# Moving the attention of the first query block into the gate stage of the second token group

## The chip, the cores and the metric

The kernel runs on one core of a Trainium2 chip. A core has five engines with an instruction queue each: TensorE (PE, matrix products), VectorE (DVE), ScalarE (ACT), GpSimd (POOL) and SyncE (SP, which issues nearly all DMAs here). Each engine takes its instructions in the order in which the program lists them, and waits on semaphores of the others. The metric is the device time of one execution in microseconds (us), and less is better.

## The reference

The reference is one step of a decoder of two layers on 2048 prompt tokens and a small sample group of 64 tokens. Each layer reads one modulated input `h`, makes four branches from it, multiplies each by its own gate, and sends all through one output product:

```python
z = h @ w_in[l]
aq, ak, av, ag, bu, bv, bg, cin, cg, dq, df, di, dg = jnp.split(z, SPLITS, axis=-1)
...
p = probs(q1, k1) - lam * probs(q2, k2)           # A: differential attention, causal, 4 heads
o_a = rms_norm(p @ v) * silu(ag)
o_c = silu(layer_norm(conv31(glu(cin)))) @ w_pw * silu(cg)   # C: depthwise convolution, 31 taps
...
mixed = jnp.concatenate([o_a, o_b, o_c, o_d], -1) @ w_out[l]
y = layer_norm(ALPHA * x + gate * mixed)
```

Branch A is the attention that the change moves. Branch C matters because its taps and its norm share the stage to which the attention is moved. Branches B (a spatial gate) and D (a linear recurrence) are untouched.

## The kernel before

A layer runs in two parts. The first part goes over the tokens in two groups of 1024, `g` = 0 and 1. For a group it makes all products with `w_in` (TensorE, three products per piece since each operand is split into a high and a low half; lines L516 to L518 and L525 to L527, accumulators `z`), keys, queries and values among them, which go to memory. The last stretch of a group is called the gate stage here: products for the gates (`gate_b`, `gate_slab`, `gate_pair`; 24 products and one `gate2` on VectorE, L195, per tile), while VectorE does the 31 taps of the convolution (`c_taps`, L1026), and then the two norms of branch C, one per 512 tokens (`c_norm`: transposes L1040, statistics L1042 to L1047, scaling L1050, transposes back L1055, tanh L1058, VectorE L1059, product L1065). In layer 0 the gate stage of `g` = 1 also makes the modulation vectors of layer 1 (`mod`, L291 to L311), whose accumulator is the single bank `X`.

The second part is the attention stage. It goes over blocks of query tiles: tiles 0 to 3, 4 to 7, 8 to 11, then 12 and 13, then 14 and 15. They are called blocks 0 to 4. `attention` loads V, and for each of four heads K and Q; for each query tile it makes two score tiles (`S`, L678), their maxima on VectorE (L682), exponentials on ScalarE (L686), the difference of the two on VectorE (L712), transposes (`T`, L725), copies (`ph`, L727) and the product with V (`X`, L730). At the end of a head ScalarE copies the sum out (`asb`), PE turns it (L741), VectorE norms it, POOL multiplies it (`ms`, L756), and it is stored in `cat`. Block 0 has 1 to 4 key tiles for its query tiles, so it is the cheapest.

The output product needs `w_out` split into two halves: `out_weights` loads sixteen pieces (`raw`, 128 x 512), ScalarE casts each (`woh`, L1306), POOL subtracts (`wol`, L172). It writes where `h` was, so it can't begin before the last product that reads that part of `h`. `out_tile` makes one tile of 128 tokens (L1354 transposes, L1373 to L1375 products, `z`); the tile of the 64 sample tokens is made first.

The order on each engine is set when the program is built: a list scheduler with its own clock takes instructions by priority, and memory that a pool gives back can be taken by the next pool as soon as its last reader is done. Nothing is reordered on the chip. The two norms have a high priority, and the order of calls in the gate stage is the string `ORD1 = 'g8 n2'`: eight gate tiles, then both norms, then the rest. `attention` draws on pools with five buffers of K, two of Q, and five and three of the exponentials.

Of the kernel before, what the change touches and what calls it, by code (L numbers as in the profile page):

```python
# [9 lines left out]
F32 = mybir.dt.float32  # L10
F32R = mybir.dt.float32r
# [13 lines left out]
P = 128  # L25
# [43 lines left out]
def hymba_step_kernel(  # L69
# [16 lines left out]
    NG = T // TG  # L86
# [8 lines left out]
              POUT=-500, PATT=0, PMOD=0, PW=0, PAV=0, PDZ=3000, PQK=500, PSL=0, PSLD=0, PPR=0, PPB=0, OT=1, GO=0, DO=0,  # L95
# [3 lines left out]
    def prio(o, f, *a):  # L99
        if not o:  # L100
            return f(*a)
        with tc.high_priority(o):
            return f(*a)
# [8 lines left out]
    NK, NMW, NPH, NP1, NP2, LEAD = (KN[k] for k in ('NK', 'NMW', 'NPH', 'NP1', 'NP2', 'LEAD'))  # L112
# [17 lines left out]
    pool = L()  # L130
# [3 lines left out]
    def nm(s):  # L134
        uid[0] += 1
        return f"{s}_{uid[0]}"
# [28 lines left out]
    def load(out, in_):  # L165
        return nc.sync.dma_start(plain(out), in_)  # L166
# [70 lines left out]
    for l in range(DEPTH):  # L237
        t = cp.tile([P, npg], I32, name=f"pidx{l}")
# [391 lines left out]
    def attention(l, t0, nt, Lx, ap, act=None):  # L630

        S = scr[l]
        prev = None
        gq, oq = divmod(t0 * P, TG)
        nkc = -(-(t0 + nt) // 4)
        while len(pool.vst) < nkc:
            vt = (ap.v if pool.vst else ap.v0).tile([P, 4, 256], F32, name=nm("V"))
            load(vt, S.vs[len(pool.vst)].rearrange("(k p) c -> p k c", p=P))
            pool.vst.append(vt)
        vst = pool.vst  # L640
        for hd in range(4):
            rows = slice(hd * 64, (hd + 1) * 64)
            kst = []
            for c in range(0, nkc * 512, 512):
                gg, o = divmod(c, TG)
                kt = ap.k.tile([P, 2, 512], F32R, tag="K", name=nm("K"), bufs=NK)
                for q, part in enumerate((0, 0, 1, 1)):
                    load(kt[q * 32:(q + 1) * 32], S.ks[gg][part][rows, o:o + 512].rearrange("(m d) t -> d m t", m=2))
                kst.append(kt)
            qt = ap.q.tile([P, 2, 512], F32R, tag="Q", name=nm("Q"), bufs=2)  # L650
            for q, part in enumerate((0, 1, 0, 1)):
                load(qt[q * 32:(q + 1) * 32, :, 0:nt * P], S.qs[gq][part][rows, oq:oq + nt * P].rearrange("(m d) t -> d m t", m=2))
            ls = smp.tile([P, 4], F32, tag="ls", name=nm("ls"), bufs=3)
            acc = None
            for j in range(nt):
                pm = prio(KN['PPB'] if t0 else KN['PPB'], attn_probs, t0 + j, qt[:, :, j * P:(j + 1) * P], kst, ls[:, j:j + 1], Lx, ap)
                if prev is not None:
                    prio(KN['PAV'], prev)
                acc = Xt() if j == 0 else acc
                prev = (lambda *a: lambda: attn_value(*a, Lx, l, ap))(t0 + j, pm, vst, acc, ls, j, nt, hd, act)  # L660
        prev()

    def attn_probs(qi, qt, kst, l1, Lx, ap):

        nk = qi + 1
        npc = -(-nk // 8)
        stt = smp.tile([P, 16], F32, tag="stt", name=nm("stt"), bufs=3)
        Pm = []
        sizes = [min(8, nk - k0) * P for k0 in range(0, nk, 8)]
        col = lambda m, j: stt[:, m * 8 + j:m * 8 + j + 1]  # L670
        for m in range(2):
            pms = []
            for pc, n in enumerate(sizes):
                s = St()
                for o in range(0, n, 512):
                    w = min(512, n - o)
                    diag = pc == npc - 1 and o + 512 >= n
                    nc.tensor.matmul(s[:, o:o + w], qt[:, m, :], kst[pc * 2 + o // 512][:, m, 0:w], start=True, stop=not diag)  # L678
                    if diag:
                        nc.tensor.matmul(s[:, o + w - P:o + w], identb, cmaskb, start=False, stop=True)  # L680

                nc.vector.tensor_reduce(col(m, pc), s[:, :n], AX.X, ALU.max, negate=True)  # L682
                if pc:
                    nc.vector.tensor_tensor(col(m, pc), col(m, pc), col(m, 0), ALU.min)  # L684
                p = (ap.p1, ap.p2)[m].tile([P, 1024], F32, tag=("P1", "P2")[m], name=nm("P"), bufs=(NP1, NP2)[m])
                nc.scalar.activation(p[:, :n], s[:, :n], AF.Exp, bias=col(m, pc), scale=1.0, accum_out=l1 if m == 0 and npc == 1 else col(m, 2 + pc))  # L686
                pms.append(p)
            lt = l1 if m == 0 and npc == 1 else col(m, 2)
            if npc > 1:

                nc.scalar.activation(col(m, 5), col(m, 0), AF.Exp, bias=col(m, 1), scale=-1.0)
                lt = col(m, 6) if m else l1
                nc.vector.scalar_tensor_tensor(lt, col(m, 2), col(m, 5), col(m, 3), op0=ALU.mult, op1=ALU.add)
            Pm.append((pms, lt))
        (p1s, lt1), (p2s, lt2) = Pm
        r = col(0, 7)
        nc.vector.reciprocal(r, lt2)
        nc.vector.scalar_tensor_tensor(r, lt1, Lx.nlam, r, op0=ALU.mult, op1=ALU.mult)
        for pc, n in enumerate(sizes):
            p1, p2 = p1s[pc], p2s[pc]  # L700
            if pc == 0 and npc > 1:
                nc.vector.tensor_tensor(col(1, 7), col(1, 5), r, ALU.mult)
                if KN['EP2']:
                    nc.gpsimd.tensor_scalar(p2[:, :n], p2[:, :n], col(1, 7), None, op0=ALU.mult)
                else:
                    nc.scalar.activation(p2[:, :n], p2[:, :n], AF.Copy, scale=col(1, 7))
                nc.vector.scalar_tensor_tensor(p1[:, :n], p1[:, :n], col(0, 5), p2[:, :n], op0=ALU.mult, op1=ALU.add)  # L707
            elif n <= KN['ECB'] * P:
                nc.scalar.activation(p2[:, :n], p2[:, :n], AF.Copy, scale=r)
                nc.gpsimd.tensor_tensor(p1[:, :n], p1[:, :n], p2[:, :n], ALU.add)  # L710
            else:
                nc.vector.scalar_tensor_tensor(p1[:, :n], p2[:, :n], r, p1[:, :n], op0=ALU.mult, op1=ALU.add)  # L712
        return p1s
# [582 lines left out]
    def out_weights(l, op):  # L1296

        O = L()
        O.op = op
# [101 lines left out]
    Lx = mod_begin(0)  # L1401
# [7 lines left out]
    for l in range(DEPTH):  # L1409
        with ExitStack() as ctx2:  # L1410
# [3 lines left out]
            for g in range(NG):  # L1414
# [38 lines left out]
                with tc.tile_pool(name=nm("cn"), reuse_waits="tile", bufs=1) as C.pool:  # L1453
# [30 lines left out]
                    for what in ORD1 if g == NG - 1 else ORD0:  # L1484
                        if what[0] == "g":
                            step(gp, int(what[1:]))
                        elif what[0] == "n":
                            norms(int(what[1:]))
                        else:
                            step(bh, int(what[1:]))  # L1490
# [11 lines left out]
        with ExitStack() as ctx2, \  # L1502
                tc.tile_pool(name=nm("pz"), reuse_waits="tile", bufs=1, space=PSUM) as pool.z, tc.tile_pool(name=nm("pT"), reuse_waits="tile", bufs=1, space=PSUM) as pool.T2:
            ap = L()
            for n in APO:
                setattr(ap, n, ctx2.enter_context(tc.tile_pool(name=nm("ap" + n), reuse_waits="tile", bufs=1)))
            op = ap.op
            if KN['WF']:
                O = prio(KN['PW'], out_weights, l, op)

            qbs = [(t, 4) for t in range(0, NT - 4, 4)] + ([(NT - 4, 2), (NT - 2, 2)], [(NT - 4, 3), (NT - 1, 1)], [(NT - 4, 2), (NT - 2, 1), (NT - 1, 1)])[KN['QB']]
            pool.vst = []
            for i, qb in enumerate(qbs):
                act = op.tile([P, qb[1], 256], F32, name=nm("act")) if i == len(qbs) - 1 else None
                if i and KN['OT'] == 0:
                    for t in range(qbs[i - 1][1]):
                        prio(KN['POUT'], out_tile, l, qbs[i - 1][0] + t, O)
                prio(KN['PATT'], attention, l, *qb, Lx, ap, act)
                if i == 0:
                    if not KN['WF']:  # L1520
                        O = prio(KN['PW'], out_weights, l, op)
                    out_gate(l, O, True)
                    out_tile(l, None, O)
                    out_gate(l, O, False)
                elif KN['OT']:
                    for t in range(qbs[i - 1][1]):
                        prio(KN['POUT'], out_tile, l, qbs[i - 1][0] + t, O)
            for t in range(qbs[-1][1]):
                out_tile(l, qbs[-1][0] + t, O, True, act[:, t])
        pool.T2 = None  # L1530
# [4 lines left out]
        Lx = NX[0]  # L1535
# [39 lines left out]
```

## Time and profile before

| | |
|---|---|
| timed, median of 3 runs | 3167.21 us (3165.14 to 3172.83) |
| the profiled execution | 3160.83 us, span 3159.1 us |
| PE busy | 2828.0 us, 90% of the span |
| VectorE busy | 2235.2 us, 71% |
| ScalarE busy | 1162.9 us, 37% |
| POOL busy | 960.8 us, 30% |

The timed runs and the profiled execution are different runs; the profiled one is 6.4 us under the median. Shares are means over the whole span. The change touches two short stretches, around 1020 us (layer 0) and around 2550 us (layer 1), so the views are read there. In a row of a timeline the first number is the start in us and the second the duration; `x4` means four instructions shown together; the square brackets give how long the engine sat idle before it, and what it waited for.

### The profile page before, as it was taken

The numbers are of one execution on the slowest core, as the hardware profiler recorded it, in microseconds if no ns is written. First come the engines' busy times: TensorE is split into PE (matmuls) and PEld (weight loads), VectorE is DVE, ScalarE is ACT, GpSimd is POOL, SyncE is SP. The second block draws the span as 40 slices with busy tenths as digits, with TensorE's granted clock in tenths as the row PEclk, the third lists the DMA queues.
The fourth block names the chain that finished last, engine by engine and source line by source line (L and its number), as shares of the span: only waits on it lengthen the run. The fifth ranks groups of instructions, "written<-read, shape, count | busy, mean of one in ns | idle before, by whom it ended". The sixth has DMA issues, their size and how long they took to land. (4 is left out here: it accounts for less than half of the span.)

```text
span 3159.1 us, 55749 instructions
## 1 busy us (share of the span) xinstructions
PE 2828.0 (90%) x20888; PEld 2254.7 (71%) x20888; DVE 2235.2 (71%) x5280; ACT 1162.9 (37%) x2452; POOL 960.8 (30%) x1061
## 2 busy tenths in 40 slices
PE   5999989898999798888979999999999988997986
PEld 3888876788876566656668888767888856665665
DVE  2567883367583788879956678833676749898897
ACT  3212223211112666666641112232110146567663
POOL 3344364312011233404253344552120031332232
PEclk8999999899999899989989999999999988998998
DMA  6433544323555754446453335444334355444652
GB/s 237 147 128 108 173 146 154 108 92 128 174 180 203 184 133 112 118 112 166 122 197 111 122 119 192 140 139 124 117 120 140 117 166 123 129 118 108 158 155 67
DMA packets 323263, 441.31 MB, mean 140 GB/s; under 512 B 58704, under 2 KB 207734, under 8 KB 315811
## 3 DMA queue, kind: packets, MB, share of 16 engines
q1 hardware_dynamic: 316850, 420.97, 44.0%
q0 software_dynamic: 6144, 16.79, 1.8%
q8 instruction: 165, 2.70, 0.4%
q14 instruction: 104, 0.84, 0.1%
HBM read 295.80 MB, written 142.05 MB: 139 GB/s over the span
## 5 line engine op out<-in xcount | busy, mean ns | idle before, releaser
L525 PE MATMUL z<-hh,wh 128*128 128x512 f32 (+1 forms) x1440 | 528.4, 367 | 17.1 <-DVE zs L195 9.1
L527 PE MATMUL z<-hh,wl 128*128 128x512 f32 (+1 forms) x1440 | 522.1, 363 | 0.0
L526 PE MATMUL z<-hl,wh 128*128 128x512 f32 (+1 forms) x1440 | 518.6, 360 | 0.0
L516 PE MATMUL z<-wh,hh 128*128 128x256 f32 (+1 forms) x1360 | 399.9, 294 | 16.0 <-ACT wh L110 4.3
L686 ACT ACTIVATE P<-S,stt 128x1024 f32<-128x1024 f32 (+7 forms) x384 | 332.7, 868 | 182.1 <-DVE stt L682 120.0
L518 PE MATMUL z<-wh,hl 128*128 128x256 f32 (+1 forms) x1360 | 394.7, 290 | 0.0
L517 PE MATMUL z<-wl,hh 128*128 128x256 f32 (+1 forms) x1360 | 393.9, 290 | 0.6 <-POOL wl L172 0.6
L682 DVE TENSOR_REDUCE stt<-S 128x1 f32<-128x1024 f32 (+7 forms) x384 | 344.0, 904 | 64.2 <-PE S L680 48.7
L1026 DVE SCALAR_TENSOR_TENSOR acc<-glu,cw,acc 128x512 f32<-128x512 f32 x480 | 378.0, 834 | 3.3
L525 PEld LDWEIGHTS z<-hh,wh 128*128 128x128 f32 x1440 | 275.7, 191 | 80.1 <-issue 14.4
L527 PEld LDWEIGHTS z<-hh,wl 128*128 128x128 f32 x1440 | 275.5, 191 | 44.7 <-issue 7.0
L526 PEld LDWEIGHTS z<-hl,wh 128*128 128x128 f32 x1440 | 275.7, 191 | 42.7 <-issue 6.3
L678 PE MATMUL S<-K,Q 128*128 128x512 f32 (+3 forms) x640 | 229.2, 430 | 77.1 <-ACT P L686 61.6
L516 PEld LDWEIGHTS z<-wh,hh 128*128 128x128 f32 (+1 forms) x1360 | 262.3, 193 | 25.9 <-issue 5.7
L517 PEld LDWEIGHTS z<-wl,hh 128*128 128x128 f32 (+1 forms) x1360 | 261.9, 193 | 4.9 <-issue 2.6
L518 PEld LDWEIGHTS z<-wh,hl 128*128 128x128 f32 (+1 forms) x1360 | 261.5, 192 | 2.3 <-issue 0.3
L172 POOL TENSOR_TENSOR wl<-raw,wh 128x512 fp32r<-128x512 f32 x112 | 150.8, 1362 | 256.5 <-ACT wh L110 218.2
L1373 PE MATMUL z<-woh,zs 128*128 128x512 f32 (+1 forms) x480 | 202.7, 422 | 24.0 <-ACT zs L110 15.1
L1375 PE MATMUL z<-woh,zs 128*128 128x512 f32 (+1 forms) x480 | 200.2, 417 | 10.0 <-POOL zs L172 9.8
L730 PE MATMUL X<-ph,V 128*64 128x128 f32 x2176 | 196.1, 294 | 10.4 <-ACT ph L727 9.8
L678 PEld LDWEIGHTS S<-K,Q 128*128 128x128 f32 x640 | 114.9, 204 | 122.1 <-ACT P L686 90.0
L725 PE MATMUL T<-cst,P 128*128 128x128 f32 x1088 | 189.2, 302 | 13.3 <-DVE P L707 8.8
(374 smaller groups left out, 5410.5 us busy)
## 6 DMA issues: line engine op xcount, KB each, us to landing
wp<-wh SPq DMA_DIRECT2D x28, 1024.0 KB
wp<-wl SPq DMA_DIRECT2D x28, 1024.0 KB
wh<-wp SPq DMA_DIRECT2D x56, 512.0 KB
wl<-wp SPq DMA_DIRECT2D x56, 512.0 KB
K<-kh SPq DMA_DIRECT2D x224, 128.0 KB
K<-kl SPq DMA_DIRECT2D x224, 128.0 KB
mw<-in_w_ada_dram SPq DMA_DIRECT2D x24, 1024.0 KB
raw<-in_w_in_dram SPq DMA_DIRECT2D x64, 256.0 KB
```

The lines of the kernel that those rows point to most:

```text
L516: nc.tensor.matmul(ps, hh[:, k, tok:tok + M], wh[:, k, :], start=(k == 0), stop=False)
L517: nc.tensor.matmul(ps, hh[:, k, tok:tok + M], wl[:, k, :], start=False, stop=False)
L518: nc.tensor.matmul(ps, hl[:, k, tok:tok + M], wh[:, k, :], start=False, stop=(k == KT - 1))
L525: nc.tensor.matmul(ps, wh[:, k, ms], hh[:, k, c0:c0 + n], start=(k == 0), stop=False)
L526: nc.tensor.matmul(ps, wh[:, k, ms], hl[:, k, c0:c0 + n], start=False, stop=False)
L527: nc.tensor.matmul(ps, wl[:, k, ms], hh[:, k, c0:c0 + n], start=False, stop=(k == KT - 1))
L678: nc.tensor.matmul(s[:, o:o + w], qt[:, m, :], kst[pc * 2 + o // 512][:, m, 0:w], start=True, stop=not diag)
L682: nc.vector.tensor_reduce(col(m, pc), s[:, :n], AX.X, ALU.max, negate=True)
L686: nc.scalar.activation(p[:, :n], s[:, :n], AF.Exp, bias=col(m, pc), scale=1.0, accum_out=l1 if m == 0 and npc == 1 else col(m, 2 + pc))
L1026: nc.vector.scalar_tensor_tensor(av, src(j), Lx.cw[:, c, j:j + 1], av, op0=ALU.mult, op1=ALU.add)
L1373: nc.tensor.matmul(po[0:M], a, wh[:, k, :], start=(i == 0), stop=False)
L1375: nc.tensor.matmul(po[0:M], b, wh[:, k, :], start=False, stop=(i == KT - 1))
```

## The change

Block 0 of the attention is called in the gate stage of `g` = 1, behind the eight gate tiles of `g8` and ahead of the two norms. It gets one small pool for everything: two buffers of K instead of five, one of Q instead of two, exponentials of 512 columns instead of 1024, three and two of them instead of five and three. The attention stage then begins with `out_weights` and the sample tile, loads V of block 0 again, and goes on with block 1. What is computed is the same.

```diff
-                kt = ap.k.tile([P, 2, 512], F32R, tag="K", name=nm("K"), bufs=NK)
+                kt = ap.k.tile([P, 2, 512], F32R, tag="K", name=nm("K"), bufs=ap.nk)
...
-            qt = ap.q.tile([P, 2, 512], F32R, tag="Q", name=nm("Q"), bufs=2)
+            qt = ap.q.tile([P, 2, 512], F32R, tag="Q", name=nm("Q"), bufs=ap.nq)
...
-                p = (ap.p1, ap.p2)[m].tile([P, 1024], F32, tag=("P1", "P2")[m], name=nm("P"), bufs=(NP1, NP2)[m])
+                p = (ap.p1, ap.p2)[m].tile([P, ap.width], F32, tag=("P1", "P2")[m], name=nm("P"), bufs=ap.np[m])
...
                     for what in ORD1 if g == NG - 1 else ORD0:
                         if what[0] == "g":
                             step(gp, int(what[1:]))
+                            if g == NG - 1:
+
+                                with ExitStack() as ctx3:
+                                    ap = L()
+                                    ap.nk, ap.nq, ap.width, ap.np = 2, 1, 512, (3, 2)
+                                    ap.k = ctx3.enter_context(tc.tile_pool(name=nm("ap"), reuse_waits="tile", bufs=1))
+                                    ap.q = ap.p1 = ap.p2 = ap.h = ap.o = ap.v = ap.v0 = ap.k
+                                    pool.vst = []
+                                    attention(l, 0, 4, Lx, ap)
...
             for i, qb in enumerate(qbs):
                 act = op.tile([P, qb[1], 256], F32, name=nm("act")) if i == len(qbs) - 1 else None
-                if i and KN['OT'] == 0:
+                if i:
+                    attention(l, *qb, Lx, ap, act)
                     for t in range(qbs[i - 1][1]):
                         prio(KN['POUT'], out_tile, l, qbs[i - 1][0] + t, O)
-                prio(KN['PATT'], attention, l, *qb, Lx, ap, act)
-                if i == 0:
-                    if not KN['WF']:
-                        O = prio(KN['PW'], out_weights, l, op)
+                else:
+
+                    O = out_weights(l, op)
                     out_gate(l, O, True)
                     out_tile(l, None, O)
                     out_gate(l, O, False)
-                elif KN['OT']:
-                    for t in range(qbs[i - 1][1]):
-                        prio(KN['POUT'], out_tile, l, qbs[i - 1][0] + t, O)
```

The call says where the work may go; the scheduler decides where it goes. Three places of the order follow, each of before and of the change apart. Numbers behind a name tell tiles apart.

**w_out, layer 0, SP.** Before, the first loads of `raw` follow the store of a gate tile (`gat_1`), ahead of the gates' end:

```order
L169 DMA gat_1_149<-zs_10065 128x512
L166 DMA V_10171<-v_0_138 128x4x256
L166 DMA raw_10749<-in_w_out_dram 128x512
L166 DMA raw_10753<-in_w_out_dram 128x512
L166 DMA raw_10757<-in_w_out_dram 128x512
L166 DMA raw_10761<-in_w_out_dram 128x512
L166 DMA lng_10813<-in_ln_g_dram 128x1024
L166 DMA lnb_10814<-in_ln_b_dram 128x1024
```

With the change they stand behind the stores of block 0's heads in `cat_0` (the four heads are ms_10034, ms_10177, ms_10320, ms_10436); only two of the sixteen are ahead of the last head's:

```order
L169 DMA cat_0_144<-ms_10177 128x4x64
L169 DMA cat_0_144<-ms_10320 128x4x64
L166 DMA raw_10753<-in_w_out_dram 128x512
L166 DMA raw_10757<-in_w_out_dram 128x512
L169 DMA cat_0_144<-ms_10436 128x4x64
L166 DMA raw_10761<-in_w_out_dram 128x512
L166 DMA raw_10765<-in_w_out_dram 128x512
```

The loads have moved from the gates to the end of block 0's attention.

**w_out, layer 0, POOL.** Before, the last of the sixteen subtracts stand ahead of the first head's multiplication (ms_10339):

```order
L172 TENSOR_TENSOR wol_10748<-raw_10797,woh_10747 128x512
L172 TENSOR_TENSOR wol_10748<-raw_10801,woh_10747 128x512
L172 TENSOR_TENSOR wol_10748<-raw_10805,woh_10747 128x512
L172 TENSOR_TENSOR wol_10748<-raw_10809,woh_10747 128x512
L756 TENSOR_TENSOR ms_10339<-ms_10339,ag_335 128x256
```

With the change all sixteen stand behind the last head's (ms_10436):

```order
L756 TENSOR_TENSOR ms_10034<-ms_10034,ag_335 128x256
L756 TENSOR_TENSOR ms_10177<-ms_10177,ag_335 128x256
L756 TENSOR_TENSOR ms_10320<-ms_10320,ag_335 128x256
L756 TENSOR_TENSOR ms_10436<-ms_10436,ag_335 128x256
L172 TENSOR_TENSOR wol_10750<-raw_10753,woh_10749 128x512
L172 TENSOR_TENSOR wol_10750<-raw_10757,woh_10749 128x512
L172 TENSOR_TENSOR wol_10750<-raw_10761,woh_10749 128x512
```

So on POOL the two have changed places.

**Block 1's first scores, layer 0, PE.** Before, they (S_10963, S_10970) lie among the last products of block 0 (S_10682, T_10668, T_10691 and X_10629 are of its last head):

```order
L741 MATMUL T_10597<-cst,asb_10595 128x64 x4
L730 MATMUL X_10629<-ph_10648,V_10171 64x128
L678 MATMUL S_10682<-K_10557,Q_10562 128x512
L680 LDWEIGHTS identb
L680 MATMUL S_10682<-cmaskb,identb 128x128
L678 MATMUL S_10963<-K_10946,Q_10956 128x512
L678 MATMUL S_10963<-K_10951,Q_10956 128x128
L680 LDWEIGHTS identb
L680 MATMUL S_10963<-cmaskb,identb 128x128
L725 MATMUL T_10668<-cst,P_10635 128x128 x2
L725 MATMUL T_10691<-cst,P_10657 128x128 x3
L678 MATMUL S_10970<-K_10946,Q_10956 128x512
```

With the change the second of them (S_10976) follows the last of 24 products of the sample tile's second half (z_10889), which read `woh` and `wol` of that half whole:

```order
L1374 MATMUL z_10889<-wol_10752,zs_10849 64x512
L1375 MATMUL z_10889<-woh_10751,zs_10850 64x512
L1373 MATMUL z_10889<-woh_10751,zs_10849 64x512
L1374 MATMUL z_10889<-wol_10752,zs_10849 64x512
L1375 MATMUL z_10889<-woh_10751,zs_10850 64x512
L678 MATMUL S_10976<-K_10952,Q_10962 128x512
L678 MATMUL S_10976<-K_10957,Q_10962 128x128
L680 LDWEIGHTS identb
```

In layer 0 block 0's first score itself (S_9880) stands three rows behind the last product of the gates, with the change as before; both norms of branch C, which before lay largely among the gates' products, now stand behind block 0.

**End of the gates, layer 1, PE.** With the change block 0 lies among the gates in this layer up to the scores of its third head (S_26364, S_26370); the last products of the gates are z_26812, and the third head's T_26334 and X_26317 follow:

```order
L741 MATMUL T_26285<-cst,asb_26283 128x64 x4
L678 MATMUL S_26364<-K_26245,Q_26250 128x512
L680 LDWEIGHTS identb
L680 MATMUL S_26364<-cmaskb,identb 128x128
L678 MATMUL S_26370<-K_26245,Q_26250 128x512
L680 LDWEIGHTS identb
L680 MATMUL S_26370<-cmaskb,identb 128x128
L526 MATMUL z_26812<-hl_21616,wh_25877 128x512
L527 MATMUL z_26812<-hh_21615,wl_25878 128x512
L996 MATMUL z_26842<-cst,glu_23643 30x128 x2
L725 MATMUL T_26334<-cst,P_26261 128x128
L730 MATMUL X_26317<-ph_26336,V_26002 64x128
```

Before, the first score of block 0 in layer 1 stood some twenty rows behind the last of the gates, with a norm between. Here too w_out's subtracts, all its loads but two, and nearly all of both norms stand with the change behind block 0's last head. On ScalarE the program has 21 loads of a function table with the change where it had 13: the eight new ones stand in this stretch, where block 0's exponentials take turns with the gelu of `gate_b`.

## Rows read from the trace of the kernel before

**Rows 1.** Windows of 25 us at both ends of the gates: busy us, clock, DMA.
```profile
core 0: us, PE busy (x) PEld busy (x) DVE busy (x) ACT busy (x) POOL busy (x), PEclk, DMA share, GB/s
1025.00:1050.00 25.00, 18.29 (x86) 11.45 (x85) 13.35 (x32) 15.20 (x43) 13.50 (x12) 0.80 1.05 276
1050.00:1075.00 25.00, 20.74 (x126) 13.95 (x127) 20.10 (x86) 14.63 (x47) 3.61 (x3) 0.93 0.82 198
2450.00:2475.00 25.00, 25.00 (x109) 20.13 (x108) 25.00 (x35) 2.40 (x4) 4.65 (x3) 1.00 0.35 113
2500.00:2525.00 25.00, 25.00 (x114) 20.07 (x112) 9.18 (x28) 4.33 (x8) 0.00 (x0) 1.00 0.41 137
2550.00:2575.00 25.00, 15.53 (x54) 8.77 (x53) 12.59 (x24) 8.98 (x17) 11.94 (x10) 0.73 0.76 196
```

**Rows 2.** Timeline of PE, layer 0: gates' last product, block 0's first score, block 1's second.
```profile
start us, us, engine line op out<-in xcount [idle before <-releaser]
1019.04 0.40 PE L527 MATMUL z<-hh,wl 128*128 128x512 f32 x1
1029.36 0.44 PE L678 MATMUL S<-K,Q 128*128 128x128 f32 x1 [3.44 <-DMA K<-kh]
...
1084.27 0.90 PE L678 MATMUL S<-K,Q 128*128 128x512 f32 x2 [0.63 <-ACT P L686]
```

**Rows 3.** Timeline of ACT, layer 0: heads' results `asb` (first and last of four).
```profile
1049.97 0.58 ACT L110 COPY asb<-X 128x512 f32<-128x512 f32 x1
...
1090.57 0.59 ACT L110 COPY asb<-X 128x512 f32<-128x512 f32 x1 [0.30 <-PE X L730]
```

**Rows 4.** Timeline of POOL, layer 0: first and last of sixteen `wol` subtracts.
```profile
1014.62 5.10 POOL L172 TENSOR_TENSOR wol<-raw,woh 128x512 fp32r<-128x512 f32 x4 [82.56 <-ACT woh L1306]
...
1053.41 1.28 POOL L172 TENSOR_TENSOR wol<-raw,woh 128x512 fp32r<-128x512 f32 x1 [1.99 <-ACT woh L1306]
```

**Rows 5.** Timeline of PE, layer 0: pieces of a norm among the gates' products.
```profile
985.05 0.44 PE L1040 MATMUL S<-cst,acc 128*128 128x128 f32 x2
986.73 1.88 PE L1065 MATMUL S<-acc,wpw 128*128 128x512 f32 x4
...
1006.81 0.27 PE L1055 MATMUL S<-cst,cn 128*128 128x128 f32 x1
```

**Rows 6.** Timeline of PE, layer 1: gates' last product, block 0's first score, block 1's second.
```profile
2554.01 0.40 PE L527 MATMUL z<-hh,wl 128*128 128x512 f32 x1
...
2572.96 1.09 PE L678 MATMUL S<-K,Q 128*128 128x128 f32 x1
...
2626.29 0.56 PE L678 MATMUL S<-K,Q 128*128 128x512 f32 x2 [0.93 <-ACT P L686]
```

**Rows 7.** Timeline of ACT, layer 1: norm 0, first casts, table load, two heads' results.
```profile
2525.93 0.78 ACT L1058 ACTIVATE cn<-S,hcn 128x512 f32<-128x512 f32 x1 [3.82 <-PE S L1055]
...
2579.06 1.28 ACT L686 ACT_TABLE_LOAD   x1
...
2611.53 0.58 ACT L110 COPY asb<-X 128x512 f32<-128x512 f32 x1
...
2632.69 0.59 ACT L110 COPY asb<-X 128x512 f32<-128x512 f32 x1 [0.32 <-PE X L730]
```

**Rows 8.** Timeline of DVE, layer 1: last statistics of norm 0.
```profile
2514.98 0.43 DVE L1042 BATCH_NORM_STATS2 cbs<-S 128x6 f32<-128x256 f32 x1 [3.56 <-PE S L1040]
```

**Rows 9.** Timeline of POOL, layer 1: eight `wol` subtracts without a wait between them.
```profile
2528.73 10.54 POOL L172 TENSOR_TENSOR wol<-raw,woh 128x512 fp32r<-128x512 f32 x8 [43.50 <-ACT woh L1306]
```

**Rows 10.** Timeline of PE, layer 0: the four kinds of product of a head.
```profile
1061.80 0.66 PE L725 MATMUL T<-cst,P 128*128 128x128 f32 x4
1064.11 0.66 PE L730 MATMUL X<-ph,V 128*64 128x128 f32 x8
1065.45 1.10 PE L741 MATMUL T<-cst,asb 128*128 128x64 f32 x8 [0.24 <-ACT asb L110]
1066.43 0.48 PE L678 MATMUL S<-K,Q 128*128 128x512 f32 x1
```

More of the change, by code (lines that the diff above doesn't have):

```diff
@@ L1504, in hymba_step_kernel @@
             ap = L()
+            ap.nk, ap.nq, ap.width, ap.np = NK, 2, 1024, (NP1, NP2)
             for n in APO:
```

## The prediction

> **What bounds the kernel now.** I began with the two stretches that the change touches, in windows of 25 us, and then read the timelines of the engines that wait there. In layer 1's gate stage PE is busy 25.00 of 25 us and VectorE too while the taps run (25.00 in the window from 2450), with ScalarE at 2.40 and POOL at 4.65 [rows 1]. So work put on PE there costs its own time, and work put on VectorE finds room only around the taps. Behind the gates neither is full: PE 18.29 and 20.74 of 25 in layer 0, 15.53 in the first window of layer 1, VectorE 12.6 to 20.1 [rows 1]. There a chain ends last: block 0's scores, maxima, exponentials, transposes, head behind head.
>
> In layer 0 the gates end at 1019.04, block 0's first score is at 1029.36 (it waited for K), and the second score of block 1 at 1084.27 [rows 2]. In layer 1 these are 2554.01, 2572.96 and 2626.29 [rows 6]. I use block 1's second score as the **mark**: from there on both kernels have the same work. From the gates' end to the mark it is 65.2 us and 72.3 us now. A head takes 13.5 us from `asb` to `asb` in layer 0 (40.6 us for three) [rows 3], and 10.6 in layer 1 (21.2 for two) [rows 7]. The reader should also see what lies in the shadow of this chain: the sixteen subtracts of w_out run from 1014.62 to 1054.69 in layer 0 [rows 4], 30 us ahead of the mark, and nobody on the path waits for the last.
>
> **The change, layer 0.** The order shows that nothing is hidden here: block 0's first score stands behind the gates' last product. What is saved in the gates is the norms' products. A norm has eight of L1040 (0.44 per two), eight of L1055 (0.27 each) and four of L1065 (1.88) [rows 5]: 5.8 us by durations. These overlap: 109 products start in 25 us, one per 0.23 [rows 1], and last 0.40 [rows 2], so I take 3.5 per norm. All of one and half of the other leave the gates: 5 us (4 to 9). Gates' end about 1014.
>
> Before, the first score came 10.3 us behind the gates [rows 2], with w_out's loads queued ahead of K and Q. With the change V, K and Q stand ahead of w_out, but still behind the stores of the gates; the one wait seen is 3.44 [rows 2]. Between 3.4 and 10.3 I take 5.5: first score at 1019.5. The first head took 20.6 us (1029.36 to 1049.97) [rows 2, 3] with much of the sample tile inside; without the 24 products of that tile's first half (0.23 each, 5.5 us) it is 15.1 at the least, and I take 17. Three more heads at between 10.6 and 13.5 I put at 11.4 each. The fourth `asb` then is at about 1070.5, 20 us earlier than now (1090.57).
>
> Now the new wait. Before, the mark stands 6.3 us *ahead* of the fourth `asb`, since block 1 begins while block 0 ends. With the change the mark stands behind the last products of the sample tile, these behind all sixteen subtracts, these on POOL behind the last head's multiplication, and their casts on ScalarE behind the first tanh of norm 0, whose last transposes stand beside the fourth `asb`. What this takes: from a norm's last statistics to the end of its first tanh 11.7 us (2514.98 to 2526.71) [rows 7, 8]; a cast, 0.6; sixteen subtracts at 1.32 (eight in 10.54) [rows 9], 21.1; the last products, 0.5. Together 34. V of block 0, loaded a second time, and block 1's K and Q have these 34 us to land in. Lower bound 28, if the norm's chain halves; upper 45, because the sixteen now take 40.1 us [rows 4], with the DMA queues full (share 1.05) [rows 1]. Queued behind them on PE is all of block 1. Mark at 1070.5 + 34 = 1104.5 against 1084.27: **+20** (+8 to +31).
>
> **The change, layer 1.** Two heads and the scores of the third lie among the gates, 2.4 heads by their work. A head's products are ten transposes (0.66 for four), twenty with V (0.66 for eight), eight of L741 (1.10) and eight scores of at most 0.48 [rows 10]: 8.3 us at most, 6.5 if scores overlap. I take 8, and as PE is full the whole of it is paid: 19 us, less 5 for the norms. Gates' end about 2568. Behind it 1.6 heads at 10.6: fourth `asb` at 2585. The same 34 us follow: 2619 against 2626.29, so -7. Against this stands PE's order: a transpose that waits for VectorE behind the taps holds up all gates behind it. 2.4 heads bring VectorE at most 25 us (an estimate from the 10.6 us at which heads follow one another), and the taps leave 0 of 25 us at their height [rows 1], though 15.8 of 25 behind them [rows 1]. Between 0 and 15 I take 4, as gate tiles lie between the pieces. **-3** (-17 to +12).
>
> The eight extra table loads are 1.28 each [rows 7], 10.3 us, on a ScalarE that is busy 2.4 of 25 us [rows 1]: I cost them at 0; with no cover they would be 10. [...]
>
> Block 0's part of `cat` is ready before block 1 begins, so its output tiles can fill PE's gaps from the start; the gaps are 4.3 of 25 us [rows 1]. **-3** for both layers (0 to -8).
>
> Sum: 20 - 3 - 3 = +14 on the profiled 3160.83, or 3175. The median of the timed runs lies 6.4 above that execution, so 3181.
>
> **Rivals.** *Faster.* The two stages have different limits, and what is taken out of the slack one costs little in the full one. This needs the pieces of layer 1 to cost 6.5 a head (15.6, gates' end at 2564.6), the rest to close in 16, and the chain behind `asb` in 28: mark at 2609, -17. Layer 0 with the gates' end at 1010, 3.4, a first head of 15.1, three of 10.6 and 28 puts the mark at 1088.3, +4; the output tiles -8. In all -21: 3146. For it speaks VectorE's 9.18 of 25 behind the taps [rows 1]. Against it speaks that w_out's sixteen subtracts alone are 21 us on one engine, in both layers. It is decided by the wait behind `asb`: at 27 us instead of 34 in both layers the sum is nothing, below that a gain. [...]
>
> *The same.* Layer 1 gives back what layer 0 loses: +12 and -10, with a few us from the output tiles: about 3167. For it speaks the opposite sign of the two terms.
>
> *Much slower.* VectorE's taps and gates hold up PE in layer 1 by 15 us, and the w_out loads take 40 us as now: +31 and +10, 3208. For it speaks that VectorE has no idle time while the taps run; against it that PE shows no wait at all in that stage now, with VectorE as full [rows 1].
>
> **How the numbers follow.** No change within 0.3% is 9.5 us, about what a measurement of this kernel can tell. The forecast (+10 to +28) has 0.43, much slower 0.12, the same 0.28, faster 0.17. So faster 0.17, same 0.28, slower 0.55. The likeliest one's own range is 3177 to 3195. The range for 8 in 10 leaves out the better half of the faster case and the upper part of the slowest: 3154 to 3205.
>
> **What would show it.** In layer 0 the first score of block 0 some 5 us behind the gates' end, the fourth `asb` near 1070, and from it 34 us to the mark, with POOL's sixteen subtracts inside and nothing on PE but the sample tile and the norms. In layer 1 the gates' end near 2570 on the old scale, PE without gaps ahead of it, and the same 34 us. It would be wrong if w_out's subtracts ran ahead of the fourth head in time, if the gates of layer 1 grew by under 10 us, or if the mark's shift in layer 0 were won back by the end of the layer.

## The result, and the profile after

The changed kernel is slower. Its median is 3221.51 us over 4 runs (3217.21 to 3222.92), against 3170.02 for the kernel before over 4 runs: a ratio of 1.0161, 95% interval 1.0143 to 1.0180. The direction was forecast, the size was not: +51 us where I had +14, outside the range (3154 to 3205) and above even the rival that I had called much slower (3208). The profiled execution took 3217.21 us with a span of 3215.4, which is 56.3 more than the span before. The terms below are taken from these two executions.

The windows of 25 us that answer to [rows 1], with two more of layer 0 (the columns are those of [rows 1]):

```profile
1025.00:1050.00 25.00, 17.45 (x82) 11.50 (x82) 15.05 (x49) 14.54 (x44) 1.46 (x2) 0.64 0.91 219
1050.00:1075.00 25.00, 21.57 (x108) 15.26 (x108) 16.61 (x70) 14.39 (x45) 1.45 (x2) 0.64 0.17 43
1075.00:1100.00 25.00, 16.53 (x62) 9.20 (x61) 14.20 (x55) 10.31 (x19) 10.46 (x9) 0.70 0.51 155
1100.00:1125.00 25.00, 19.30 (x65) 9.52 (x64) 9.83 (x25) 11.20 (x20) 11.85 (x10) 0.86 0.75 204
2500.00:2525.00 25.00, 25.00 (x115) 19.79 (x115) 25.00 (x41) 12.07 (x19) 3.47 (x2) 1.00 0.52 148
2550.00:2575.00 25.00, 25.00 (x113) 20.35 (x112) 8.34 (x18) 3.74 (x10) 0.00 (x0) 1.00 0.39 131
```

In layer 1 the interleaving works as the change intends: from 2500 to 2525 PE stays at 25.00 of 25 while VectorE, which was at 9.18 there, is also at 25.00. In layer 0 no engine is full behind the gates: from 1075 on, where the kernel before is past its mark by 1084, PE is at 16.53 and 19.30 of 25, VectorE at 14.20 and 9.83, ScalarE and POOL below 12. The granted clock is at 0.64 in the two windows where it was at 0.80 and 0.93.

The timeline of PE, the lines that answer to [rows 2, 6] and what lies between block 0's last head and the mark in layer 0; 1670.01 is layer 1's first product:

```profile
1016.44 0.39 PE L527 MATMUL z<-hh,wl 128*128 128x512 f32 x1
...
1025.50 0.45 PE L678 MATMUL S<-K,Q 128*128 128x128 f32 x1 [7.27 <-DMA K<-kh]
...
1088.33 0.78 PE L1373 MATMUL z<-woh,zs 128*64 128x512 f32 x1
...
1097.30 3.44 PE L1065 MATMUL S<-acc,wpw 128*128 128x512 f32 x4 [2.52 <-ACT cn L110]
...
1101.48 0.44 PE L1040 MATMUL S<-cst,acc 128*128 128x128 f32 x2 [0.29 <-DVE cbs L1042]
...
1107.97 1.69 PE L1055 MATMUL S<-cst,cn 128*128 128x128 f32 x4 [2.14 <-ACT cn L1050]
...
1114.21 0.90 PE L678 MATMUL S<-K,Q 128*128 128x512 f32 x2
...
1118.23 0.45 PE L1373 MATMUL z<-woh,zs 128*64 128x512 f32 x1 [1.17 <-DVE t L1377]
...
1120.58 1.88 PE L1065 MATMUL S<-acc,wpw 128*128 128x512 f32 x4
...
1125.52 0.46 PE L678 MATMUL S<-K,Q 128*128 128x512 f32 x2
...
1670.01 0.38 PE L516 MATMUL z<-wh,hh 128*128 128x256 f32 x1
...
2608.33 0.40 PE L527 MATMUL z<-hh,wl 128*128 128x512 f32 x1
...
2675.50 0.45 PE L678 MATMUL S<-K,Q 128*128 128x512 f32 x2
```

The same product of layer 1 in the kernel before, in the timeline of PE:

```profile
1625.66 0.39 PE L516 MATMUL z<-wh,hh 128*128 128x256 f32 x1 [0.31 <-ACT zs L476]
```

So layer 0 ends 44.35 us later (1670.01 less 1625.66), and the mark in it stood already 41.25 later (1125.52 against 1084.27 in [rows 2]). In layer 1 the gates end at 2608.33, the mark is at 2675.50. Less the 44.35 inherited, that is +9.97 and +4.86 against [rows 6]; the other 7.1 us of the 56.3 come behind layer 1's mark.

ScalarE's timeline answers to [rows 3, 7]: the fourth `asb` is at 1079.16 and 2628.90. In layer 0 the three heads behind the first take 36.95 us (1042.21 to 1079.16), less than the 40.6 before, so the small pool does not slow them there.

```profile
1042.21 0.58 ACT L110 COPY asb<-X 128x512 f32<-128x512 f32 x1
...
1079.16 0.58 ACT L110 COPY asb<-X 128x512 f32<-128x512 f32 x1 [0.76 <-PE X L730]
...
1083.39 1.93 ACT L1050 ACTIVATE cn<-S,smc,smcy 128x256 f32<-128x256 f32 x4 [1.63 <-DVE smc L1047]
...
1086.56 1.13 ACT L1306 CAST woh<-raw 128x512 fp32r<-128x512 f32 x2
...
1096.14 0.62 ACT L1306 CAST woh<-raw 128x512 fp32r<-128x512 f32 x1 [5.51 <-DMA raw<-in_w_out_dram]
1096.67 0.58 ACT L110 COPY cn<-S 128x512 f32<-128x512 f32 x1
...
1105.27 0.62 ACT L1306 CAST woh<-raw 128x512 fp32r<-128x512 f32 x1 [3.87 <-DMA raw<-in_w_out_dram]
...
1107.36 1.92 ACT L1050 ACTIVATE cn<-S,smc,smcy 128x256 f32<-128x256 f32 x4
...
1122.56 0.59 ACT L110 COPY cn<-S 128x512 f32<-128x512 f32 x1 [4.78 <-PE S L1065]
...
2488.84 0.60 ACT L895 ACTIVATE zs<-z 128x512 f32<-128x512 f32 x1
2489.45 1.28 ACT L686 ACT_TABLE_LOAD   x1
2490.75 0.58 ACT L686 ACTIVATE P<-S,stt 128x384 f32<-128x384 f32 x1
...
2628.90 0.58 ACT L110 COPY asb<-X 128x512 f32<-128x512 f32 x1 [0.76 <-PE X L730]
```

POOL's first and last of the sixteen subtracts in layer 0, which answer to [rows 4]:

```profile
1087.24 5.85 POOL L172 TENSOR_TENSOR wol<-raw,woh 128x512 fp32r<-128x512 f32 x4 [1.27 <-ACT woh L1306]
...
1114.97 4.98 POOL L172 TENSOR_TENSOR wol<-raw,woh 128x512 fp32r<-128x512 f32 x4 [1.14 <-DMA raw<-in_w_out_dram]
```

From the fourth `asb` to the mark it is 46.4 us in layer 0 and 46.6 in layer 1, where I had 34. The reader should see two chains side by side in these 46 us. **The norms**: norm 0 scales at 1083.39, and norm 1 at 1107.36, 24 us later, since both go through the same score tiles (`S`, two buffers) in the order of the program; the last copy out of one is at 1122.56, and only then is that buffer free for block 1. **w_out**: the first casts are at 1086.56, the subtracts run from 1087.24 to 1119.95 with ScalarE waiting 5.51 and 3.87 us for `raw`, and the 24 products of the sample tile's second half begin at 1118.23 and end where the mark stands. These 24 waited for VectorE's L1377, which frees the sample tile's one accumulator (`z`), and that in turn for a subtract, since it writes to one of the four buffers of `raw`; in VectorE's timeline:

```profile
1117.49 0.68 DVE L1377 TENSOR_TENSOR t<-z,gate 64x512 f32<-64x512 f32 x1 [1.39 <-POOL wol L172]
```

The two chains also meet: at 1096.14 a cast that waits for `raw` stands ahead of norm 0's copy (1096.67) on ScalarE, and PE's L1065 at 1097.30 waits for that copy.

### The profile page after: what moved, and what is told of

The parts are those of the page before. It is cut to its first block, busy times and chain, and to the rows that moved or that the text cites. A ratio compares the mean times of both kernels' runs of the same rounds, so it can differ in the third digit from the quotient of the medians.

```text
span 3215.4 us, 55790 instructions
## 1 busy us (share of the span) xinstructions
PE 2850.6 (89%) x20888; PEld 2264.4 (70%) x20888; DVE 2213.6 (69%) x5280; ACT 1174.6 (37%) x2460; POOL 962.8 (30%) x1061
## 5 line engine op out<-in xcount | busy, mean ns | idle before, releaser
L727 ACT COPY ph<-T 128x512 f32<-128x512 f32 (+2 forms) x320 | 160.0, 521 | 156.6 <-PE T L725 155.4
L730 PE MATMUL X<-ph,V 128*64 128x128 f32 x2176 | 202.8, 300 | 11.5 <-ACT ph L727 9.2
```

The costliest lines, as they stand in the source:

```text
L730: nc.tensor.matmul(acc[e * 64:(e + 1) * 64, j4 * P:(j4 + 1) * P], vst[c // 4][:, j, hs], ph[:, j, :], start=(c + j < 2), stop=(c + j >= nk ...
```

## The experiments

On the three chips of these runs the kernel before took 3170.64, 3188.84 and 3197.47 us (medians), so each kernel is compared with runs of the kernel before on its own chip, as a ratio; times are given as differences inside one execution. My account at this point was that the loss is made behind block 0's last head, in layer 0 above all, by the norms and by w_out; the other accounts are named in the expectations.

**One layer alone.** The call stays in the gate stage for one layer, and the other does block 0 in the attention stage (with the small pool's call left out there):

```diff
-                            if g == NG - 1:
+                            if g == NG - 1 and l == 0:
...
+                    if not (l == 0):
+                        attention(l, *qb, Lx, ap, act)
```

> Block 0 moved in layer 0 only; layer 1 as before. Theory A (the loss is what stands behind block 0's last head: both norms, w_out's sixteen pieces, the sample tile; in layer 0 nothing is hidden for it): the trace of the changed kernel puts 44 us of its 56 into layer 0, so 3214 us, +44. Theory B (the small pool slows the heads, in both layers alike): about +25 in each layer, 3195.

Measured: 1.0127 (1.0096 to 1.0157), about +40 us of the 51, near what theory A has. The fourth `asb` to the mark took 49.4 us.

The same edit with `l == 1`:

> Block 0 moved in layer 1 only; layer 0 as before. Theory A: in layer 1 about as much is hidden as is lost behind the last head, +5 to +12: 3175 to 3182. Theory B: +25, 3195.

Measured: 1.0031 (1.0006 to 1.0056), about +10 us; `asb` to mark 51.3 us in layer 1. The two parts add up to the whole, four fifths of it in layer 0, so there is no cost that only both together have, and theory B, with as much in either layer, is out.

**The norms ahead of block 0.** The call of block 0 moves behind `norms(...)` in the same loop:

```diff
                             step(gp, int(what[1:]))
+                        elif what[0] == "n":
+                            norms(int(what[1:]))
                             if g == NG - 1:
...
-                        elif what[0] == "n":
-                            norms(int(what[1:]))
```

> The changed kernel with block 0 called behind the two norms instead of ahead of them, in both layers. By the order the norms lie among the gates again as before, nothing of block 0 is hidden in either layer, and w_out's pieces still stand behind its last head. Theory A: layer 0 gains the norms' part of the 46 us between the last head and block 1's second score, some 15 us; layer 1 loses the 2.4 hidden heads and gains the same 15. In sum +30 to +45: 3200 to 3215. If the norms' place were the whole of the loss, it would be within 10 us of the kernel before.

Measured: 1.0286 (1.0255 to 1.0317), worse than the change itself; this expectation missed. The fourth `asb` in ScalarE's timeline, and PE's first product with `woh` behind it and the mark:

```profile
1094.34 0.58 ACT L110 COPY asb<-X 128x512 f32<-128x512 f32 x1 [1.22 <-PE X L730]
```

```profile
1115.43 0.69 PE L1373 MATMUL z<-woh,zs 128*64 128x512 f32 x1 [9.74 <-ACT woh L1306]
...
1126.95 0.88 PE L678 MATMUL S<-K,Q 128*128 128x512 f32 x2
```

With the norms out of the way it is still 32.6 us from `asb` to mark (32.8 in layer 1), now with PE waiting 9.74 us for a cast of w_out. So without the norms w_out holds block 1 for some 30 us; the last wait in layer 1 is 3.58 us for Q. What is worse than in the change is layer 1, where no head is hidden among the gates any more: from the layer's first product to its mark it takes 1053.1 us (1676.85 to 2729.96), and 1023.7 with the change in layer 1 alone on the same chip (1637.64 to 2661.37).

**w_out's memory apart.** The pool that holds `woh`, `wol` and `raw` is opened ahead of the attention's, so that it no longer falls on the memory of block 0's small pool:

```diff
-APO='o k p2 h p1 v v0 op q'
+APO='op o k p2 h p1 v v0 q'
```

> The changed kernel with the pool of w_out's pieces and of the output tile first in the attention stage's memory, so that it takes the memory of the gates' weights and not that of block 0's small pool. By the order w_out's loads and subtracts then stand at the gates' end as in the kernel before; norms still behind block 0. Theory A: the 33 us of subtracts leave the chain, what stays are the norms (about 20 us behind the last head): 20 to 30 us less in each layer, 3165 to 3185. Theory B or any cause in block 0's own heads: no change, 3221.

Measured: 1.0218 (1.0185 to 1.0250); missed as well. In PE's timeline the norm's last product, block 1's first score and the mark:

```profile
1144.51 1.98 PE L1065 MATMUL S<-acc,wpw 128*128 128x512 f32 x4 [0.15 <-ACT cn L110]
...
1152.91 0.70 PE L678 MATMUL S<-K,Q 128*128 128x512 f32 x2 [3.15 <-DMA K<-kl]
...
1160.32 0.84 PE L678 MATMUL S<-K,Q 128*128 128x512 f32 x2
```

And the norm's last copy out of `S`, in ScalarE's timeline:

```profile
1146.53 0.59 ACT L110 COPY cn<-S 128x512 f32<-128x512 f32 x1 [0.74 <-PE S L1065]
```

The fourth `asb` is at 1107.82, so the mark is 52.5 us behind it (65.8 in layer 1). In layer 0 the last subtract of w_out ends at 1073.06, ahead of that `asb`, so what follows is the price of the norms without w_out: their last copy ends at 1147.12, 39.3 us behind the `asb`. Behind them block 1's first score waits 3.15 us for K, and products of an output tile stand ahead of the second. Why K comes late is not shown. In layer 1 the edit does not clear w_out: its last subtract ends at 2674.31, 15 us behind the `asb`. Taking away one chain shows the other.

**w_out with four loads instead of sixteen**, every fourth piece loaded and used four times (the rows of `w_out` are wrong for twelve of sixteen pieces):

```diff
-                raw = op.tile([P, 512], F32, tag="xs", name=nm("raw"), bufs=4)
-                load(raw, w_out[l, kk * P:(kk + 1) * P, j * 512:(j + 1) * 512])
+                raw = op.tile([P, 512], F32, tag="xs", name=nm("raw"), bufs=4) if kk % 4 == 0 else raw
+                if kk % 4 == 0:
+                    load(raw, w_out[l, kk * P:(kk + 1) * P, j * 512:(j + 1) * 512])
```

> The changed kernel with one load of w_out for four pieces (the other twelve pieces of a layer are made from the wrong rows, so the output product has wrong weights; casts, subtracts and products are all there). The changed kernel's sixteen subtracts take 32.7 us in layer 0 where 21.1 was predicted, with waits for loads between. If the loads set that pace, they now take 21 to 23, and about 10 us are won in each layer: ratio 1.009 to 1.012. If something else holds block 1 up (the norms, the single output accumulator), 1.014 to 1.016.

Measured: 1.0138 (1.0111 to 1.0165). ScalarE's fourth `asb`, POOL's sixteen subtracts and PE's mark:

```profile
1073.86 0.58 ACT L110 COPY asb<-X 128x512 f32<-128x512 f32 x1 [0.76 <-PE X L730]
```

```profile
1081.95 20.66 POOL L172 TENSOR_TENSOR wol<-raw,woh 128x512 fp32r<-128x512 f32 x16 [1.26 <-ACT woh L1307]
```

```profile
1120.36 0.56 PE L678 MATMUL S<-K,Q 128*128 128x512 f32 x2 [0.26 <-ACT cn L110]
```

The subtracts now take 20.66 us in one piece, the 21.1 of my sum, and are over at 1102.61. The mark does not move: 46.5 us behind `asb` (45.0 in layer 1). It waits for the norm's last copy (`ACT cn L110`), 18 us after w_out is done. So the loads had only set the pace of w_out's chain, and here the norms end last. But w_out still lengthens them. VectorE works out norm 1's scale in small steps on 128 x 4 values, and these take 1.2 us each while POOL subtracts, and 0.16 when it has stopped:

```profile
1094.04 1.21 DVE L179 TENSOR_SCALAR smci<-smc 128x4 int32<-128x4 int32 x1
...
1101.44 1.19 DVE L189 SCALAR_TENSOR_TENSOR smca<-smca,smcy 128x4 f32<-128x4 f32 x1
1102.66 0.16 DVE L190 SCALAR_TENSOR_TENSOR smcy<-smca,smcy 128x4 f32<-128x4 f32 x1
```

From L1045 to L1047 the steps take 10.2 us (1093.42 to 1103.60), where the change has 2.5 (1102.64 to 1105.18). Without these 7.6 us the mark would be some 39 us behind `asb` (an estimate), which agrees with the 39.3 of the run before.

**Both removed.** The norms ahead of block 0, with w_out's four loads:

> Block 0 behind the norms, and one load of w_out for four pieces (twelve pieces of a layer are made from the wrong rows, so the output product has wrong weights). With the norms out of the way the subtracts should set block 1's start: sixteen in 21 us instead of some 33, and block 1's second score 20 to 26 us behind the fourth head's result instead of 33. With the norms behind the head the same edit moved it by nothing (46.5 against 46.4).

Measured: 1.0229 (1.0198 to 1.0261) over two runs; `asb` to mark 28.1 and 25.9 us, with the subtracts at 19.70. The gain over the norms ahead alone (32.6) is small, as the casts still begin only behind the last head, and block 1's first score now waits for Q (5.32 and 3.58 us). Then the norms ahead of block 0, with w_out's memory apart, and as a control that second edit on the kernel before:

> Both earlier edits at once in the changed kernel, in both layers: block 0 called behind the norms, and the pool of w_out's pieces first in the attention stage's memory. By the order the norms and w_out's loads then stand where the kernel before has them; block 0 still has its small pool and stands behind the gates, V is loaded twice. Theory A' (two chains stand behind block 0's last head, the two norms through the score banks, 46 us, and w_out's pieces, 33 us; each alone holds block 1 up, so that each edit alone won little): now both are gone, and most of the +0.029 and +0.022 of the single edits with them: ratio to the kernel before 0.998 to 1.010. Rival (the small pool, or V's second load): 1.015 or more.

> The kernel before with only the pool of w_out's pieces first in the attention stage's memory: what that order of memory costs or brings by itself. Theory A' has it at 0.997 to 1.005.

Measured: 1.0101 (1.0077 to 1.0125), and 1.0057 (1.0032 to 1.0082) for the control, a little above what I expected of either, and the rival (1.015 or more) is out. Less the control, some 0.44% of loss is left of the change. ScalarE's fourth `asb` and PE's first two scores of block 1:

```profile
1114.36 0.59 ACT L110 COPY asb<-X 128x512 f32<-128x512 f32 x1 [1.22 <-PE X L730]
```

```profile
1127.08 0.87 PE L678 MATMUL S<-K,Q 128*128 128x512 f32 x2 [10.12 <-DMA Q<-ql]
1127.85 0.88 PE L678 MATMUL S<-K,Q 128*128 128x512 f32 x2
```

From `asb` to mark it is 13.5 us in both layers, and 10.12 of it is a wait for Q, 10.08 in layer 1. By the order in which the pools are opened Q is now the one that takes memory of block 0's small pool; that it waits for that was not tried by itself. The wait behind the head has fallen by 33 us in each layer, and the ratio by less than that (from 1.0161 to 1.0101), because nothing of block 0 is hidden in layer 1 any more: the fourth `asb` is 1027.3 us behind the layer's first product here, 1024.6 in the control and 958.9 in the change.

The time from the fourth `asb` of block 0 to the mark, in us:

| kernel | layer 0 | layer 1 | what is left of the queues |
|---|---|---|---|
| before [rows 2, 3, 6, 7] | -6.3 | -6.4 | none |
| before, w_out's memory apart | -9.4 | -4.8 | none |
| the change | 46.4 | 46.6 | norms and w_out |
| four loads | 46.5 | 45.0 | norms, lengthened by w_out at 21 us |
| norms first | 32.6 | 32.8 | w_out (layer 1: then Q) |
| norms first, four loads | 28.1 | 25.9 | w_out at 20 us, then Q |
| w_out's memory apart | 52.5 | 65.8 | norms, then K (layer 1: some of w_out too) |
| norms first, w_out's memory apart | 13.5 | 13.5 | Q |

**The modulation later.** In layer 0 the modulation products of layer 1 hold the bank `X`, which block 0 needs; here they come behind the call:

```diff
-MO=0
+MO=2
```

> The changed kernel with the modulation vectors of layer 1 made behind the gates instead of ahead of them. By the order block 0 of layer 0 then lies among the gates up to its third head, as in layer 1. If layer 0 loses more than layer 1 because nothing of block 0 is hidden there (theory A), its loss falls from some 40 us to the 10 of layer 1, plus what the vectors' products cost behind the gates (24 products and their loads, up to 10): ratio to the kernel before 1.005 to 1.009 instead of 1.016. If the loss of layer 0 lies elsewhere, 1.016 stays.

Measured: 1.0134 (1.0099 to 1.0170), against the 1.0161 of the change; the intervals overlap, and it is less than I expected. The heads do go among the gates: the fourth `asb` of block 0 is at 1018.80 instead of 1079.16, 60 us earlier. But block 1's first head has its `asb` at 1135.49, 24 us earlier than the change's 1159.63, and layer 1 begins at 1652.33, 18 earlier. POOL's first subtracts of w_out show where it went:

```profile
1104.22 5.28 POOL L172 TENSOR_TENSOR wol<-raw,woh 128x512 fp32r<-128x512 f32 x4 [78.56 <-ACT woh L1306]
```

They waited until 1104.22, 85 us behind the last head: SP issues the first loads of `raw` at 1100.77, behind the stores of the modulation's last results (1098.52). What the heads gained, the modulation and w_out behind it took.

**Fewer heads among the gates, layer 1 alone.** `attention` gets the heads to do; the first two, or the first alone, in the gate stage, the others in the attention stage, layer 0 as before:

```diff
-    def attention(l, t0, nt, Lx, ap, act=None):
+    def attention(l, t0, nt, Lx, ap, act=None, heads=range(4)):
...
-        for hd in range(4):
+        for hd in heads:
...
-                                    attention(l, 0, 4, Lx, ap)
+                                    attention(l, 0, 4, Lx, ap, None, range(2))
...
+                    attention(l, *qb, Lx, ap, act, range(2 if l == 1 else 0, 4))
```

> Only layer 1, and only the first two heads of block 0, in the gate stage; heads three and four stay in the attention stage, and layer 0 is as before. By the order w_out's loads then start at the gates' end and block 1 follows the fourth head as in the kernel before; norm 1 is behind the gates. Theory A (hiding as such is worth a little, the loss is what stands behind the last head): the gates grow by 13 to 16 us, the stage behind them shrinks by two heads, 21, and gets 5 of norm: -5 to 0 us. If hiding heads among the gates costs as such: +5 or more.

> The same with one head: the norms stay among the gates as in the kernel before. Theory A: gates +7, behind them -10: -3 us, hardly to be told from no change. If hiding costs as such: +3 or more.

Measured: 1.0039 (1.0020 to 1.0058) for two heads, 1.0017 (1.0003 to 1.0032) for one; some 12 and 5 us. Both missed theory A, which had a gain, and came out as the other branch has it, that hiding costs as such; the second can hardly be told from no change, with an interval that begins at 1.0003. With one head the queues behind block 0 are as before (the mark at 2635.97 is 4.5 us *ahead* of the fourth `asb`). So a head hidden among the gates brings nothing in the sum, even without the queues, and not all of layer 1's loss is made behind the last head. Which part of the layer takes it back these two runs don't settle, and I leave it open.

None of the versions beats the kernel before. A pool for Q of its own, and `raw` loaded by another queue than SP's, were not tried.

## Why the prediction was right or wrong

**The failed step: the 34 us** from the fourth `asb` to the mark. It measured 46.4 and 46.6, over my upper bound of 45, so the two layers lost 25 us more than I had. I had put the two queues in a row, and counted only the first half of one norm (11.7 us) before w_out's 21.1. They run side by side, and each is longer than I had it: the norms are two in series through the buffers of `S` (39 us without w_out, by layer 0 of the run with w_out's memory apart), and w_out's subtracts take 32.7 us, paced by the loads (32.6 to the mark, by the run with the norms first). And they lengthen each other, so that 39 and 33 make 46: a cast that waits 5.51 us for `raw` stands ahead of a norm's copy on ScalarE (1096.14 and 1096.67), and VectorE's L195 in norm 0 takes 1.52 and 1.59 us while POOL subtracts (1087.54 and 1090.37), where in norm 1, between two subtracts, it takes 0.69 (1111.36 and 1114.19). In the run with four loads norm 1's small steps took 1.2 us too instead of 0.16; in the change POOL is idle beside them, and they take 2.5 us in all. That block 1 is queued behind them was right, and so was where they begin. What I missed is that the score tiles are shared: I read who waits for an engine, and not who holds the buffer.

**Layer 0, up to the fourth `asb`.** Three small terms, all on the same side, each under the 8.1 us over which the four runs of the kernel before spread (3165.14 to 3173.24). The gates saved 2.6 us instead of 5 (1019.04 to 1016.44). The first score came 9.1 us behind them instead of 5.5, with 7.27 of it a wait for K. The first score to the fourth `asb` took 53.7 instead of 51. Together 8.7, and with 12.4 from the failed step they make the mark's +41.25 out of the +20, but for rounding.

**Layer 1, the gates.** +9.97 where I had 14 for the gates and 4 for a stall of PE behind VectorE. The stall did not come: between 2440 and 2610 the waits of PE come to 0.8 us, though VectorE is at 25.00 of 25 from 2500 to 2525. So the rival that VectorE holds up PE is out. My own sign of an error, gates that grow by under 10 us, was met by a hair: this was the part that came out cheaper. Gates' end to the fourth `asb` took 20.6 instead of 17. With the 12.6 of the failed step the mark came to +4.86 instead of -3.

**The table loads at nothing**: right. Gelu starts at 2488.84 for 0.60, the load at 2489.45 for 1.28, and the next exponential at 2490.75: the whole switch is 1.31 us here. PE's only wait for ScalarE between 2440 and 2610 was 0.8 us.

**Output tiles early, -3**: wrong. From the mark to the end it was +3.1 us in layer 0 and +7.1 in layer 1. The output tiles of block 0 do fill PE from the start of block 1, and delay its first head: the mark to the first `asb` of block 1 takes 34.1 us (1125.52 to 1159.63) where it took 22.5 (1084.27 to 1106.80). That they are the cause of the whole 10 us is argued and not shown.

Summed over the two profiled executions: 21.25 for layer 0's mark, 7.9 for layer 1's and 13.2 behind the marks, added to the +14, give the 56.3.

**The rivals.** *Faster* needed 27 us or less behind `asb` in both layers; only the kernels without the norms there came to it, and they had paid for it earlier. That work taken out of a slack stage costs little in a full one was my argument for it. In layer 1 the edit did fill PE and VectorE both (25.00 of 25 from 2500 to 2525); but there the whole edit measured 1.0031, and one head alone 1.0017, so no run here bears the gain out. *The same* fell with layer 0. *Much slower* (3208) came nearest to the size: of its two causes slow loads of w_out were there (subtracts of 32.7 us, though not 40), and a VectorE that holds up PE was not.

## What to carry to other kernels

Before a stage is moved ahead of another, list what it holds while it runs: accumulator buffers (PSUM), SBUF, and places in the queues. What came behind it here and needed these was delayed to its end, high priority or not: two norms and sixteen loads, hidden before, stood in the 46 us behind the last head. When two such queues run side by side, taking one away wins little: price each alone, expect more than the longer where they share engines (here 39 and 33 made 46), and test by removing both.

## What the hardware showed that I had not expected

The same products cost PE more time. Both kernels have 20888 of them; PE's busy time is 2850.6 us now (first part of the page) and was 2828.0:

```profile
PE 2850.6 (89%) x20888; PEld 2264.4 (70%) x20888; DVE 2213.6 (69%) x5280; ACT 1174.6 (37%) x2460; POOL 962.8 (30%) x1061
```

The granted clock was lower too: over the execution it is 0.940 now and 0.951 before. Behind the gates of layer 0 it is at 0.64 from 1025 to 1075, while block 0's heads run by themselves, and at 0.70 from 1075 to 1100, in the window in which PE waits for the two queues. A product of the sample tile takes 0.78 us at 1088.33, where the granted clock was 0.50 (window 1087.00 to 1089.20), and 0.45 at 1118.23, where it was 1.00 (1118.20 to 1118.70); four of L1065 take 3.44 us at 1097.30, behind a wait of 2.52, at a clock of 0.57 (1097.30 to 1100.70), and 1.88 at 1120.58, at 1.00 (1120.50 to 1122.50). So this stretch cost PE more than its waits: these products ran slowly too. What set the clock is not shown.

VectorE's small steps took 1.2 us instead of 0.16 while POOL subtracted, in the run with four loads. The kernel before has it too, 8.6 us ahead of its mark in layer 0: three steps in a row (L190, L183, L189) take 1.25, 1.20 and 1.20 us from 1075.62 on, while POOL runs L1390 and L1391 (1075.60 to 1079.32), and the next L190, at 1079.37, takes 0.16. The statistics of the norm (L1042) kept their 0.43 us beside a subtract (at 1100.99 in the change, the subtract from 1100.70 to 1101.97).

On SP's queue a late store stood ahead of loads. The first two loads of `raw` are issued at 1080.85 and the next two at 1086.43, each pair right behind a store of a head in `cat` that waited for POOL's L756, 15.0 us for the two stores. Whether the loads could have gone earlier without them is not shown. ScalarE's later wait of 5.51 us for `raw` (1096.14) is not of this kind: the fifth load, which takes a buffer over from the first subtract, was issued at 1089.20, and that cast is the fifth.
